# An encoder step in split fp32 products: input loaded in place, weights of the retention output loaded ahead, one tile with priority, the last products in a written order

## The chip, the cores and the metric

The kernel runs on one core of one Trainium2 chip. The core has five engines with instruction streams of their own: TensorE (PE), which multiplies matrices, VectorE (DVE), ScalarE (ACT), GpSimd (POOL) and SyncE (SP), which here issues most DMA transfers. They wait for one another through semaphores. The metric is the device time of one execution in microseconds (us). A kernel's time is the median of its runs.

## The reference

One step of a one-layer streaming encoder: 1024 prompt tokens and 64 sample tokens, width 1024. Cut to what matters:

```python
def mixer_prompt(h, g_attn, w_in, ...):
    rq, rk, rv, rg, sq, sk, sv, ga, gb = split(rms_norm(h, g_attn) @ w_in)
    q, k, v = retention_qkv(rq, rk, rv, pos)                  # rotary
    st, o = scan(retention_block, s0, chunks(q, k, v))        # 4 heads, chunks of 64
    swa_o = swa_attend(sq, band(sk), band(sv), bias, sinks)   # window 128
    a = (rms_norm(o) * silu(rg)) @ w_ret_out
    b = swa_o @ w_swa_out
    return (sigmoid(ga) * a + sigmoid(gb) * b) @ w_mix_out
...
h = h + mixer(h)                                    # prompt and sample, with their caches
h = h + cross_attn(rms_norm(h, g_cross), mk, mv)    # 4 heads, 256 memory tokens, then @ w_co
hn = rms_norm(h, g_ffn)
h = h + (silu(hn @ w_gate) * (hn @ w_up)) @ w_down  # D_FF = 2816
y = rms_norm(h, g_final)                            # h * rsqrt(mean(h*h) + 1e-6) * g_final
```

Everything is float32. Outputs are y for prompt and sample tokens, the retention states, the window's keys and values, and the memory's keys and values.

## The kernel before

**Products.** All 1088 tokens stand as columns (T = 1088; a half is 544, a quarter HC = 272; CH = 384, 384, 320). Activations are kept with features on the 128 partitions, so a unit of work is a 128x128 weight block against some hundred token columns. Each fp32 operand is split into a high part, cast to the type that TensorE takes (fp32r), and a low part, the rest: `split` (L122) is an ACT cast (L123) and a DVE subtraction (L124). A product is three matmuls, high by high, high by low, low by high (`mm3`, L147, and `multiply`, L199, lines 205, 206 and 208). The large products (in-projection, gate, up, down) are Strassen products (`strassen`): of a weight pair and operand blocks B11, B12, B21, B22 (features by token halves) seven products are made with sums T1 to T4 of the blocks; the weights' sums are made on POOL (`weight_ops`, L183 to L189).

**Order.** The instructions are written for all engines in one program, and a scheduler sets the order on each engine. `high_priority()` lets instructions pass others, `issue_after(x)` holds an instruction until x has been issued. SP issues loads and stores in order, and an entry that waits for a buffer holds what is behind it.

**Start** (`start_phase`, L403). The x columns are loaded by half and feature block, 16 pieces of 128x544, into the staging tile xr with four buffers; ACT multiplies each by the gain g into xg (L428). From xg `operands_early` splits B11 and B12, `operands_late` splits B21 and B22, and `first_sums` and `put_sum` (L1280) subtract on DVE and split T1 = B12 − B11, T2 = B22 − T1, T3 = T2 − B11 and T4 = B21 − T2, in place in xg's quarters. With w_v's blocks (`plain_weights`) the first products follow.

**Filler** (`filler`, L1042). While the window attention (SWA) runs, whose matmuls are small, this generator yields larger products between its steps. Its first loop (`operands`) loads the retention result d_gate[0], 8 feature blocks by three column chunks, each load held until `self.loaded`, the last weight load so far, and splits it into `rets`. Then come the last memory head's values, and then w_ret_out block by block: `unit` = `unit_raw` (a load of 512 KB into the staging tile "raw", two buffers) and `unit_parts` (the splits). The SWA's tokens are loaded after `operand_loaded`, the last load of the first chunk.

**Cross output** (`cross_out_phase`, L1219). For each block m of w_co and each chunk a dense product is added to the residual (L1241), stored, multiplied by the FFN's gain and the norm of before (L1244) into xg, and its squares are added into rstd_f (`add_square`, L278). After the last block the norm follows: a product with ones (L306), roots, and a product that spreads them over partitions (L330).

**Tail** (`down`, L1412). The last group of w_down's products leaves out P2 and P4 of the Strassen scheme; instead 16 plain products of 128x272 (nine matmuls each) are made at the end, eight for the first quarter of columns, eight for the second. Each is added to y (L1506) and passed to `complete` (L1441): square on ACT, add to rstd on DVE (L1450), multiply y by the final gain on ACT (L1451). After the first eight, `final_norm` is called for the second half (columns 544 to 1087) and for the first quarter, after the last eight for the second quarter: matmuls with ones (L306), roots on 128 x few columns (`rsqrt`, L284), a spreading product (L1527) and a copy (L1528). `final_scale` multiplies y by it on DVE (L1533) and stores.

## Time and profile before

| | |
|---|---|
| median of 3 runs | 2258.14 us (2256.48 to 2258.49) |
| the profiled execution | 2251.97 us |
| its span, first to last instruction | 2250.1 us |
| mean granted TensorE clock | 0.988 |
| PE busy, DVE busy | 97%, 71% of the span |
| bytes moved by DMA | 290.84 MB, mean 129 GB/s |

The profile is that of one execution. Busy time is given by engine; the matmuls' ends are modelled, so a busy PE isn't PE at its peak. In a group of instructions the row reads line, engine, operation, output and inputs, shapes and count, then busy time and mean ns of one, then the idle time of the engine ahead of them and what ended most of it. In a timeline the row begins with the start and the duration in us from the span's start. In the table of waits a row names what waited, what it waited for, the total in us, how often, and the longest. L12 is line 12 of the kernel.

### The profile page before, as it was taken

To read this page: it belongs to the slowest core of one execution; us is meant where nothing else is said; L and a number is where in the kernel's file an instruction comes from. 1 tells how busy PE (TensorE), PEld (TensorE's weight loads), DVE (VectorE), ACT (ScalarE), POOL (GpSimd) and SP (SyncE) were. 2 spreads that over 40 slices of the span, in tenths; PEclk is the share of its full clock that TensorE was granted. 3 is DMA by queue.
4 is the path that set the end of the run, shared out by engine and by line. 5 is a ranking of instruction groups with operands and counts; after the bars stand their busy time and mean duration, and the time that the engine had idled before them with its cause. 6 is when DMAs were issued, how large, how long until landed. Compare 5 with 4: busy or idle time off the path is not lost.

```text
span 2250.1 us, 41674 instructions
## 1 busy us (share of the span) xinstructions
PE 2172.4 (97%) x16382; PEld 2108.2 (94%) x16382; DVE 1594.2 (71%) x2656; ACT 896.2 (40%) x1921; POOL 689.0 (31%) x466
## 2 busy tenths in 40 slices
PE   7899999999999989999999999999999999999996
PEld 6899999999999977779999998999999999999996
DVE  8985878677687568875455565776777767777596
ACT  7333333435444355553233343333222223344344
POOL 1441534342253112220000000014555556434471
PEclk9999999999999989999999999999999999999997
DMA  5433344443445475326343111412342332475223
GB/s 199 159 120 109 111 129 130 132 130 113 169 139 187 143 242 164 111 67 222 121 153 113 39 66 59 143 62 91 122 148 79 101 131 85 152 258 192 86 84 108
DMA packets 182598, 290.84 MB, mean 129 GB/s; under 512 B 40290, under 2 KB 110850, under 8 KB 182402
## 3 DMA queue, kind: packets, MB, share of 16 engines
q1 hardware_dynamic: 177794, 279.26, 38.2%
q10 hardware_dynamic: 4608, 8.91, 1.1%
q8 instruction: 129, 2.11, 0.4%
q14 instruction: 67, 0.55, 0.1%
HBM read 196.95 MB, written 91.16 MB: 128 GB/s over the span
## 4 chain that ended last, share of the span: by engine, by line
PE 80%; DVE 10%; DMA 4%; issue 3%; ACT 2%; POOL 1%; SPq 0%; DVEq 0%; ACTq 0%; POOLq 0%
PE pq L205 15%; PE pq L208 15%; PE pq L206 15%; PE pd L149 8%; PE pd L150 8%; PE pd L151 8%; DVE wq L124 2%; PE pout L992 1%; PE pp L976 1%; DMA hl<-d_op 1%; PE pss L934 1%; DVE T L124 1%; DVE B L124 1%; PE pk L691 1%; DVE xg L1280 1%
## 5 line engine op out<-in xcount | busy, mean ns | idle before, releaser
L123 ACT CAST wq<-raw 128x512 fp32r<-128x512 f32 (+1 forms) x505 | 307.9, 614 | 572.1 <-PE pq L208 308.2
L124 DVE TENSOR_TENSOR wq<-raw,wq 128x512 fp32r<-128x512 f32 (+1 forms) x505 | 447.6, 890 | 107.7 <-ACT wq L123 105.7
L205 PE MATMUL pq<-T,wq 128*128 128x272 f32 x1832 | 501.3, 291 | 6.4 <-DVE u L252 3.1
L206 PE MATMUL pq<-T,wq 128*128 128x272 f32 x1832 | 497.7, 288 | 0.0
L205 PE MATMUL pq<-B,wq 128*128 128x272 f32 x1592 | 436.7, 292 | 11.7 <-ACT wq L123 10.5
L206 PE MATMUL pq<-B,wq 128*128 128x272 f32 x1592 | 435.1, 290 | 9.1 <-DVE B L124 8.9
L208 PE MATMUL pq<-T,wq 128*128 128x272 f32 x1832 | 382.6, 289 | 1.0 <-DVE wq L124 0.9
L183 POOL TENSOR_TENSOR raw<-raw 128x512 f32<-128x512 f32 (+1 forms) x59 | 81.6, 1383 | 899.7 <-DVE wq L124 615.2
L205 PEld LDWEIGHTS pq<-T,wq 128*128 128x128 f32 x1832 | 345.2, 188 | 7.2 <-DVE u L252 3.2
L206 PEld LDWEIGHTS pq<-T,wq 128*128 128x128 f32 x1832 | 348.5, 190 | 0.3 <-issue 0.3
L208 PE MATMUL pq<-B,wq 128*128 128x272 f32 x1592 | 333.5, 289 | 0.0
L206 PEld LDWEIGHTS pq<-B,wq 128*128 128x128 f32 x1592 | 304.4, 191 | 11.7 <-DVE B L124 11.3
L205 PEld LDWEIGHTS pq<-B,wq 128*128 128x128 f32 x1592 | 301.3, 190 | 12.4 <-ACT wq L123 10.5
L208 PEld LDWEIGHTS pq<-T,wq 128*128 128x128 f32 x1832 | 285.3, 188 | 2.4 <-DVE wq L124 1.7
L208 PEld LDWEIGHTS pq<-B,wq 128*128 128x128 f32 x1592 | 249.1, 189 | 0.5 <-issue 0.3
L252 DVE TENSOR_TENSOR u<-pq,u 128x544 f32<-128x544 f32 x177 | 127.7, 721 | 128.2 <-PE pq L208 127.5
L186 POOL TENSOR_TENSOR raw<-raw 128x512 f32<-128x512 f32 (+1 forms) x59 | 83.5, 1415 | 141.0 <-DVE wq L124 133.4
L563 DVE TENSOR_TENSOR stage<-pq,u 128x544 f32<-128x544 f32 x112 | 80.4, 718 | 29.1 <-PE pq L208 26.5
L962 POOL TENSOR_TENSOR t<-t,den 128x768 f32<-128x768 f32 (+2 forms) x34 | 47.9, 1409 | 167.5 <-DVE nm L950 58.7
L184 POOL TENSOR_TENSOR raw<-raw 128x512 f32<-128x512 f32 (+1 forms) x59 | 88.3, 1497 | 3.7
L1438 POOL TENSOR_TENSOR y<-u,y 128x544 f32<-128x544 f32 x38 | 63.0, 1664 | 73.6 <-DVE y L1436 51.8
L189 POOL TENSOR_TENSOR raw<-raw 128x512 f32<-128x512 f32 (+1 forms) x59 | 84.1, 1426 | 4.4
(356 smaller groups left out, 4669.8 us busy)
## 6 DMA issues: line engine op xcount, KB each, us to landing
hl<-d_op SPq DMA_DIRECT2D x85, 272.0 KB, 4.1
d_qkv<-stage SPq DMA_DIRECT2D x44, 272.0 KB, 2.1
d_op<-stage SPq DMA_DIRECT2D x44, 272.0 KB, 2.1
d_op<-ht SPq DMA_DIRECT2D x44, 272.0 KB, 3.3
raw<-w_gate SPq DMA_DIRECT2D x22, 512.0 KB, 3.4
raw<-w_up SPq DMA_DIRECT2D x22, 512.0 KB, 3.5
d_gate<-stage ACTq DMA_DIRECT2D x32, 272.0 KB, 2.3
raw<-w_down SPq DMA_DIRECT2D x16, 512.0 KB, 4.3
```

What stands on the lines that cost most here:

```text
L123: self.last_cast = self.nc.scalar.copy(hi, src).ins
L124: self.nc.vector.tensor_tensor(out=lo, in0=src, in1=hi.bitcast(F32), op=ALU.subtract)
L149: mm(ps, wh, xh, start=start, stop=False)
L150: mm(ps, wh, xl, start=False, stop=False)
L151: self.last_mm = mm(ps, wl, xh, start=False, stop=stop).ins
L184: tt(out=a21, in0=a21, in1=a22, op=add)
L186: tt(out=a11, in0=a22, in1=a11, op=sub)
L189: tt(out=a12, in0=a12, in1=a11, op=sub)
L205: mm(ps[:, c, :HC], w[:, 0, ks], x[:, 0, cs], start=start, stop=False)
L206: mm(ps[:, c, :HC], w[:, 0, ks], x[:, 1, cs], start=False, stop=False)
L208: self.last_mm = mm(ps[:, c, :HC], w[:, 1, ks], x[:, 0, c * HC:(c + 1) * HC], start=False, stop=stop).ins
L252: add = lambda out, a, b: nc.vector.tensor_tensor(out=out, in0=a, in1=b, op=ALU.add)
```

## The change

Four edits.

1. Start: the 16 pieces of x are loaded straight into xg, and ACT no longer multiplies them by g there. The operands B11 to B22 are made with the gain: high part = x times g on ACT, low part = x times g minus the high part in one DVE instruction (scalar_tensor_tensor). The sums take the gain in as well; gneg holds −g. `first_sums` isn't used here any more.
2. Filler: the load of w_ret_out's first block is written ahead of the loads of the retention operands; its splits stay where they were. As `unit_raw` sets `self.loaded`, the operands' loads are now held until this load.
3. Cross output: the last block's steps behind the product are emitted with high priority.
4. Tail: the last 16 products and everything behind them are written in `finish`, in a fixed order. `queued` holds each DVE instruction until the one before it in this list has been issued; `in_order` does the same for PE. The norm of the second half is taken during the first eight products and the following (sums after product 5, spread after 7), that of the first quarter after products 11 and 14. The final gain is no longer multiplied on ACT but by the scaling itself. For the second quarter the sum over partitions is written 128 rows wide (a product with a 128x128 of ones, over the accumulated squares and the last square), and the roots are taken on 128x272.

```diff
...
         self.last_cast = self.nc.scalar.copy(hi, src).ins
-        self.nc.vector.tensor_tensor(out=lo, in0=src, in1=hi.bitcast(F32), op=ALU.subtract)
+        return self.nc.vector.tensor_tensor(out=lo, in0=src, in1=hi.bitcast(F32), op=ALU.subtract).ins
...
         self.early = [sp.tile([P, 2, HC], F32, name=f"early{i}") for i in range(4)]
-        xr = lambda: sp.tile([P, HALF], F32, tag="xr", bufs=4, name="xr")
+        self.gneg = self.np.tile([P, KT], F32, name="gneg")
+        nc.vector.tensor_scalar(self.gneg, g, -1.0, None, ALU.mult)
         raws = [self.wp.tile([P, 1024], F32, tag="raw", bufs=2, name="raw") for i in range(2)]
...
             for k in range(k0, k0 + 4):
-                x = xr()
-                self.load(x, io["xT"][k, :, hs])
-                nc.scalar.mul(self.xg[k][:, hs], x, g[:, k:k + 1])
+                self.load(self.xg[k][:, hs], io["xT"][k, :, hs])
...
                 columns(n)
-            if n == 1:
-                self.operands_early()
         self.load(self.ident, io["c_ident"])
-        w = self.plain_weights(raws)
-        self.operands_late(self.first_sums)
-        return w
+        self.start_operands()
+        return self.plain_weights(raws)
+    def start_operands(self):
+        nc = self.nc
+        g, stt = self.gains[:, 0, :], nc.vector.scalar_tensor_tensor
+        self.op_tiles(0, ("B11", "T1"))
+        self.ops["B12"] = [self.b12[:, k] for k in range(4)]
+        self.op_tiles(1, ("B21", "B22", "T2", "T3"))
+        self.op_tiles(0, ("T4",))
+        col = lambda t, k: t[:, k:k + 1]
+        qs = [self.quarters(k) for k in range(4)]
+        for i, name in enumerate(("B11", "B12", "B21", "B22")):
+            for k in range(4):
+                o, x, gk = self.ops[name][k], qs[k][i], col(g, k + i // 2 * 4)
+                nc.scalar.mul(o[:, 0], x, gk)
+                stt(o[:, 1], x, gk, o[:, 0].bitcast(F32), ALU.mult, ALU.subtract)
+        for k, (b11, b12, b21, b22) in enumerate(qs):
+            nc.vector.tensor_tensor(out=b12, in0=b12, in1=b11, op=ALU.subtract)
+            nc.scalar.mul(b12, b12, col(g, k))
+            self.put_op("T1", k, b12)
+        for k, (b11, b12, b21, b22) in enumerate(qs):
+            stt(b12, b22, col(g, k + 4), b12, ALU.mult, ALU.subtract)
+            self.put_op("T2", k, b12)
+        for k, (b11, b12, b21, b22) in enumerate(qs):
+            stt(b11, b11, col(self.gneg, k), b12, ALU.mult, ALU.add)
+            self.put_op("T3", k, b11)
+        for k, (b11, b12, b21, b22) in enumerate(qs):
+            stt(b21, b21, col(g, k + 4), b12, ALU.mult, ALU.subtract)
+            self.put_op("T4", k, b21)
...
+            first = self.unit_raw(io["w_ret_out"][0], KT)
             for c0, n in CH:
...
             for m in range(KT):
-                u = self.unit(io["w_ret_out"][m], KT)
+                u = self.unit(io["w_ret_out"][m], KT) if m else self.unit_parts(first, KT)
                 for c0, n in CH:
...
                 ps = self.dense(u, self.couts, c0, n)
-                nc.vector.tensor_tensor(out=x, in0=ps, in1=x, op=ALU.add)
-                self.store(self.d_h[1][m, :, c0:c0 + n], x)
-                acc = self.rstd_f[:, c0:c0 + n]
-                nc.vector.scalar_tensor_tensor(self.xg[m][:, c0:c0 + n], x, self.gains[:, 2, m:m + 1],
-                                               self.rstd[:, c0:c0 + n], ALU.mult, ALU.mult)
-                self.add_square(acc, x, m == 0, cq, n)
+                with tc.high_priority() if m == KT - 1 else nullcontext():
+                    nc.vector.tensor_tensor(out=x, in0=ps, in1=x, op=ALU.add)
+                    self.store(self.d_h[1][m, :, c0:c0 + n], x)
+                    acc = self.rstd_f[:, c0:c0 + n]
+                    nc.vector.scalar_tensor_tensor(self.xg[m][:, c0:c0 + n], x, self.gains[:, 2, m:m + 1],
+                                                   self.rstd[:, c0:c0 + n], ALU.mult, ALU.mult)
+                    self.add_square(acc, x, m == 0, cq, n)
                 if m == KT - 1:
...
-    def operands_late(self, sums=None):
+    def operands_late(self):
         self.op_tiles(1, ("B21", "B22", "T2", "T3"))
...
             self.put_op("B22", k, b22)
-        if sums is not None:
-            sums()
         for k, (b11, b12, b21, b22) in enumerate(qs):
...
                 nc.vector.tensor_tensor(out=acc, in0=acc, in1=sq, op=ALU.add)
-            nc.scalar.mul(o, o, self.gains[:, 3, m:m + 1])
...
             q = self.rings[ring].tile("wb", slot=slots[m // 2 % 2])
-            self.split(raw[:, :2 * n], q[:, 0, :2 * n], q[:, 1, :2 * n])
+            self.last_queued = self.split(raw[:, :2 * n], q[:, 0, :2 * n], q[:, 1, :2 * n])
             rest += [(m + i, q[:, :, i * n:(i + 1) * n], self.ops[("B21", "T4")[i]]) for i in range(2)]
-        for c0 in (0, HC):
-            for m, q, xs in rest:
-                ps = self.ps.tile([P, 2, 512], F32, tag="q", name="pq")[:, 0, :HC]
-                for k, x in enumerate(xs):
-                    ks = slice(k * P, (k + 1) * P)
-                    x = x.rearrange("p a (b c) -> p a b c", b=2)[:, :, c0 // HC]
-                    self.mm3(ps, q[:, 0, ks], q[:, 1, ks], x[:, 0], x[:, 1], k == 0, k == len(xs) - 1)
-                v = y[m][:, c0:c0 + HC]
-                nc.vector.tensor_tensor(out=v, in0=ps, in1=v, op=ALU.add)
-                complete(m, c0, HC)
-            if c0 == 0:
-                self.final_norm(HALF, HALF)
-                self.final_scale(y, HALF, HALF)
-            self.final_norm(c0, HC)
-        for c0 in (0, HC):
-            self.final_scale(y, c0, HC)
-
-    def final_norm(self, c0, n):
+        self.finish(y, rest)
+    def queued(self, emit):
+        with self.tc.issue_after(self.last_queued):
+            self.last_queued = emit().ins
+    def finish(self, y, rest):
         nc = self.nc
-        acc = self.rstd[:, c0:c0 + n]
-        spans = self.spans(n)
-        with self.tc.high_priority():
+        tt, stt, ts = nc.vector.tensor_tensor, nc.vector.scalar_tensor_tensor, nc.vector.tensor_scalar
+        cols = [slice(0, HC), slice(HC, HALF), slice(HALF, T)]
+        squares, factors = {}, {}
+        bank = lambda: self.bank_pair()[:, 0, :]
+        def product(c, m, q, xs):
+            ps = bank()[:, :HC]
+            for k, x in enumerate(xs):
+                ks = slice(k * P, (k + 1) * P)
+                x = x.rearrange("p a (b c) -> p a b c", b=2)[:, :, c]
+                self.mm3(ps, q[:, 0, ks], q[:, 1, ks], x[:, 0], x[:, 1], k == 0, k == len(xs) - 1)
+            return ps
+        def grow(c, m, ps):
+            v = y[m][:, cols[c]]
+            self.queued(lambda: tt(out=v, in0=ps, in1=v, op=ALU.add))
+            sq = self.rstd[:, cols[c]]
+            if m:
+                sq = self.hl.tile([P, HALF], F32, tag="hl", name="sq")[:, :HC]
+            nc.scalar.activation(sq, v, AF.Square)
+            squares[c, m] = sq
+        def gather(c, m):
+            acc = self.rstd[:, cols[c]]
+            self.queued(lambda: tt(out=acc, in0=acc, in1=squares[c, m], op=ALU.add))
+        def sums(c):
+            spans = self.spans(cols[c].stop - cols[c].start)
+            ps = bank()[:, :2 * len(spans)].rearrange("p (t two) -> p t two", two=2)
+            for i, (a, w) in enumerate(spans):
+                a += cols[c].start
+                self.last_mm = nc.tensor.matmul(ps[:, i, :], self.rstd[:, a:a + w], self.ones[:, :2], start=True, stop=True).ins
             r = self.np.tile([P, 5], F32, tag="rf", bufs=2, name="rs_f")[:, :len(spans)]
-            self.token_rstd(r, [acc], spans, D)
-            for a, b in ((0, 2), (2, 5)) if n > 512 else ((0, len(spans)),):
-                pb = self.norm_psum("pb")
-                a0, a1 = spans[a][0], spans[b - 1][0] + P
-                for i in range(a, b):
+            factors[c] = r, spans, ps[:, :, 0]
+        def roots(c):
+            r, spans, ps = factors[c]
+            v = self.np.tile([P, 5], F32, tag="vf", bufs=2, name="rf_v")[:, :len(spans)]
+            t = self.np.tile([P, 5], F32, tag="tf", bufs=2, name="rf_t")[:, :len(spans)]
+            self.steps(r, v, t, ps)
+        def wide_roots(c, m):
+            ps = bank()[:, :HC]
+            mm = nc.tensor.matmul
+            mm(ps, self.ones, self.rstd[:, cols[c]], start=True, stop=False)
+            self.last_mm = mm(ps, self.ones, squares[c, m], start=False, stop=True).ins
+            v, t = (self.hl.tile([P, HALF], F32, tag="hl", name="wide")[:, :HC] for _ in range(2))
+            self.steps(self.rstd[:, cols[c]], v, t, ps)
+        def spread(c):
+            r, spans, _ = factors[c]
+            for part in ((0, 2), (2, 5)) if len(spans) > 4 else ((0, len(spans)),):
+                pb = bank()
+                a0, a1 = spans[part[0]][0], spans[part[1] - 1][0] + P
+                for i in range(*part):
                     at = spans[i][0] - a0
-                    nc.tensor.matmul(pb[:, at:at + P], r[:, i:i + 1].broadcast_to([P, P]), self.ident, start=True, stop=True)
-                nc.scalar.copy(acc[:, a0:a1], pb[:, :a1 - a0])
-
-    def final_scale(self, y, c0, n):
+                    self.last_mm = nc.tensor.matmul(pb[:, at:at + P], r[:, i:i + 1].broadcast_to([P, P]), self.ident,
+                                                    start=True, stop=True).ins
+                c0 = cols[c].start
+                nc.scalar.copy(self.rstd[:, c0 + a0:c0 + a1], pb[:, :a1 - a0])
+        def scale(c, k):
+            o = y[k][:, cols[c]]
+            self.queued(lambda: stt(o, o, self.gains[:, 3, k:k + 1], self.rstd[:, cols[c]], ALU.mult, ALU.mult))
+            self.store(self.io["o_y"][k, :, cols[c]], o)
+        for j in range(2 * KT):
+            c, m = divmod(j, KT)
+            ps = self.in_order(lambda: product(c, *rest[m]))
+            grow(c, rest[m][0], ps)
+            if (j - 1) % KT and j:
+                gather((j - 1) // KT, rest[(j - 1) % KT][0])
+            if j == 5:
+                self.in_order(lambda: sums(2))
+                roots(2)
+            if j == KT - 1:
+                self.in_order(lambda: spread(2))
+            if j == KT + 3:
+                self.in_order(lambda: sums(0))
+                roots(0)
+            if j == KT + 6:
+                self.in_order(lambda: spread(0))
+            if j >= KT:
+                scale(2, j - KT)
+        for k in range(3):
+            scale(0, k)
+        self.in_order(lambda: wide_roots(1, rest[-1][0]))
+        for k in range(3, KT):
+            scale(0, k)
         for k in range(KT):
-            o = y[k][:, c0:c0 + n]
-            self.nc.vector.tensor_tensor(out=o, in0=o, in1=self.rstd[:, c0:c0 + n], op=ALU.mult)
-            self.store(self.io["o_y"][k, :, c0:c0 + n], o)
+            scale(1, k)
+    def steps(self, out, v, t, ps):
+        nc = self.nc
+        stt, q = nc.vector.scalar_tensor_tensor, self.queued
+        q(lambda: nc.vector.tensor_scalar(v, ps, 1.0 / D, EPS, ALU.mult, ALU.add))
+        nc.scalar.activation(out, v, AF.Sqrt)
+        q(lambda: nc.vector.reciprocal(out, out))
+        q(lambda: nc.vector.tensor_tensor(out=t, in0=out, in1=out, op=ALU.mult))
+        q(lambda: stt(t, t, -0.5, v, ALU.mult, ALU.mult))
+        q(lambda: stt(out, t, 1.5, out, ALU.add, ALU.mult))
...
```

`in_order` is a method that the kernel has already; it holds PE's instructions behind `self.last_mm`.

2 lines of the change are left out of this document (1 added, 1 removed).

## The prediction

> **What bounds the kernel now.** I read the page's first part, then the waits of TensorE (PE) in the four places that the change touches, then a timeline of each.
>
> ```profile
> span 2250.1 us, 41674 instructions
> PE 2172.4 (97%) x16382; PEld 2108.2 (94%) x16382; DVE 1594.2 (71%) x2656; ACT 896.2 (40%) x1921; POOL 689.0 (31%) x466
> PE pq L205 <- ACT wq L123: 10.5, 1, 10.5
> PE pq L206 <- DVE B L124: 5.5, 3, 2.6
> PE pb L815 <- ACT ret_o L811: 5.1, 5, 1.4
> PE pd L149 <- ACT wq L123: 8.6, 2, 5.8
> PE pt L306 <- DVE rstd_f L278: 3.6, 1, 3.6
> PE pb L1527 <- DVE rs_f L294: 5.3, 3, 2.7
> ```
>
> PE is busy 97% of the span, so all that any change of order can give back is 2250.1 − 2172.4 = 77.7 us. The six rows of waits (total, times, longest) lie, in order, at 0–60 us (two rows), 120–560, 815–880, 1460–1540 and 2130–2251 us: the start, retention, the filler's output weights, the cross output and the tail. Each part of the change aims at one of them, the third row excepted. No matmul work is removed anywhere, so the gain cannot be more than these waits and what comes before and behind them.
>
> **Start.** The matmuls wait for operands, and VectorE (DVE) makes the operands.
>
> ```profile
> 5.00:10.00 5.00, 0.00 (x0) 0.00 (x0) 1.48 (x3) 4.99 (x9) 0.00 (x0) 1.00 0.94 312
> 80.00:90.00 10.00, 9.77 (x79) 9.77 (x79) 10.00 (x15) 3.58 (x6) 3.05 (x3) 1.00 0.46 158
> 5.64 1.39 ACT L428 ACTIVATE xg<-xr,gains 128x544 f32<-128x544 f32 x2
> 6.93 0.63 ACT L123 CAST B<-xg 128x544 fp32r<-128x544 f32 x1
> 7.59 0.72 DVE L124 TENSOR_TENSOR B<-xg,B 128x544 fp32r<-128x544 f32 x1 [6.58 <-ACT B L123]
> L124 DVE TENSOR_TENSOR T<-xg,T 128x544 fp32r<-128x544 f32 x16 | 13.5, 871 | 0.7 <-ACT T L123 0.7
> L124 DVE TENSOR_TENSOR B<-xg,B 128x544 fp32r<-128x544 f32 x12 | 9.7, 807 | 7.5 <-ACT B L123 7.5
> L124 DVE TENSOR_TENSOR b<-xg,b 128x544 fp32r<-128x544 f32 x4 | 2.9, 722 | 0.7 <-ACT b L123 0.7
> L269 DVE SCALAR_TENSOR_TENSOR xc<-ld,gains,xc 128x384 fp32r<-128x384 f32 x16 | 9.9, 619 | 11.0 <-ACT xc L268 11.0
> L124 DVE TENSOR_TENSOR mix<-ld,mix 128x384 fp32r<-128x384 f32 x16 | 8.9, 558 | 8.1 <-ACT mix L123 8.1
> ```
>
> In a table by slices the columns are PE, its loads, DVE, ACT and POOL, each busy us (instructions), then granted clock, DMA share and GB/s. DVE is the limit: once it runs, at 7.59, it is full, still 10.00 of 10.00 us at 80–90. So the stage shortens by what DVE gains, not by the 10.5 us that PE waits.
> - DVE begins sooner. Now ACT multiplies x by g (two in 1.39 us from 5.64), casts (6.93), and only then DVE subtracts (7.59). After, the product of x and g is itself the high part: the first DVE instruction follows one 0.7 us multiplication, at about 6.4. −1.2 us.
> - DVE idles less. The three L124 groups hold 0.7 + 7.5 + 0.7 = 8.9 us of idle time, of which 6.58 is the first wait: 2.3 are left, all behind ACT. ACT drops from 48 instructions on x (16 multiplications, 32 casts) to 36, and x no longer waits for four staging buffers. About 0.4 stays: −1.9 us.
> - DVE's instructions grow. The count stays 48 (32 splits, 16 subtractions), but 28 become scalar_tensor_tensor with a gain per partition: 16 for the B blocks, 4 each in the sums T2, T3, T4. At equal shape that form takes 619 against 558 ns: 28 × 0.061 = +1.7 us, and gneg once, about 0.1.
> - The built program's order puts two more retention instructions (about 0.7 us each) on DVE ahead of PE's wait near 98 us. They are only brought forward; this stands in the bound.
>
> Sum −1.2 − 1.9 + 1.8 = **−1.3**. Bounds: −3.6 (all idle goes, no surcharge) to +1 (1.2 of the idle stays, and the two instructions are not made good).
>
> **Retention, 110–560 us.** The start shifts how weights' products and retention are interleaved; no work changes. The third row of waits is what can move: a transposition (pb) waits for the norm of its head. There are 20 such places, five wait 1.0–1.4 us now. In the new order the number of matmuls between a head's last product and its pb falls from 89 to 68 at the first place and rises at thirteen of the others. I take 0, bounds −5.1 (none waits) to +5 (ten wait).
>
> **Filler.** The load of w_ret_out[0] moves ahead of the retention operands.
>
> ```profile
> 809.83 12.77 SPq L117 DMA_DIRECT2D swin<-d_gate  x7
> 831.35 0.81 SPq L117 DMA_DIRECT2D raw<-w_ret_out  x2
> 820.40 2.50 DVE L124 TENSOR_TENSOR wq<-raw,wq 128x512 fp32r<-128x512 f32 x4 [1.81 <-ACT wq L123]
> 831.58 0.27 PE L911 MATMUL pd<-ident,swin 128*128 128x128 f32 x1
> 837.65 0.69 PE L149 MATMUL pd<-ret,wq 128*128 128x384 f32 x1 [5.79 <-ACT wq L123]
> 842.33 0.52 PE L151 MATMUL pd<-ret,wq 128*128 128x384 f32 x1
> 845.15 0.34 PE L149 MATMUL pd<-ret,wq 128*128 128x384 f32 x1
> 820.00:825.00 5.00, 4.43 (x19) 4.14 (x20) 4.53 (x13) 4.91 (x11) 0.00 (x0) 0.50 0.90 283
> 825.00:830.00 5.00, 4.79 (x39) 4.52 (x38) 3.19 (x9) 2.75 (x12) 0.77 (x1) 0.89 1.04 384
> 830.00:835.00 5.00, 1.38 (x13) 1.05 (x13) 4.69 (x17) 4.27 (x19) 0.62 (x1) 0.79 0.93 330
> ```
>
> The load is issued at 831.35, because in the program it stands behind the loads of the gates; PE stands still for 5.79 us. After, the load stands near the head of SP's queue, but it needs a staging buffer that the split at 820.40 frees, at about 821.7. SP issues in order, so the seven gate loads that now go out from 809.83 to 822.6, and everything else behind, wait for it too: the one on which PE's next instruction depends (token v, transposed at 831.58) comes last. From 821.7 until then some 3.8 MB must come in (0.5 of weights, nine gate loads of 0.2, the window's queries 1.0, its keys and values 0.5). At the 330–384 GB/s of the last two slices that is 10–11.5 us: PE's transposition moves from 831.58 to about 834, and the output products, which follow it, start there and not at 837.65. **−2.8**, since the weights are long there. What is late next: DVE (4.69 of 5.00 busy at 830–835) with the gate splits. Bounds: −5 (the idle time falls to 2.4 us) and 0 (the splits that were covered by the stall are on the path).
>
> After the stall twelve matmuls run at half pace (0.52 us at 842.33, 0.34 at 845.15): 12 × 0.18 = 2.2 us that a shorter stall might save. A wait of 2.8 us (8.6 less 5.8 in the L149 row) ahead of 820.4 was followed by a granted clock of 0.50, so I count nothing for it. By the Trainium skill, "TensorE: Matmul & The Clock Gate", "What's actually happening", an idle window of some 3.4 us halves the clock, free-running; with 2.4 us left the sum would be about 2 us better by the rule; the trace's 2.8 us with a clock of 0.50 behind it speak against counting on it.
>
> **Cross output.** The 3.6 us wait on L278 has its cause on DVE, where the last tile's chain queues behind splits. In the built program the order on DVE, ACT and PE in this stage is the same as before, instruction by instruction: the priority is set on instructions that the tile's own products already release late. **0**, bounds −0.3 to +0.3.
>
> **Tail.** The last 16 products get a written order, with the norm of each third between them; scaling becomes one instruction; the last third's root is taken over the full width.
>
> ```profile
> 2217.84 1.17 PE L306 MATMUL pt<-ones,rstd 128*128 128x2 f32 x10
> 2225.19 1.62 PE L1527 MATMUL pb<-ident,rs_f 128*128 128x128 f32 x6 [2.68 <-DVE rs_f L294]
> 2226.46 0.57 PE L149 MATMUL pq<-B,wb 128*128 128x272 f32 x1
> 2236.51 0.29 PE L151 MATMUL pq<-T,wb 128*128 128x272 f32 x1
> 2244.12 3.55 SPq L120 DMA_DIRECT2D o_y<-y  x7
> 2224.96 1.35 DVE L1533 TENSOR_TENSOR y<-y,rstd 128x544 f32<-128x544 f32 x2
> 2243.56 2.55 DVE L1533 TENSOR_TENSOR y<-y,rstd 128x272 f32<-128x272 f32 x7
> L1533 DVE TENSOR_TENSOR y<-y,rstd 128x272 f32<-128x272 f32 x14 | 5.1, 437 | 0.0
> L787 PE MATMUL pos<-state,qsm 128*64 128x256 f32 x16 | 4.3, 392 | 0.0
> L1149 DVE RECIPROCAL cden<-cden 128x2 f32<-128x2 f32 x16 | 2.6, 165 | 8.5 <-ACT p L1147 8.5
> L291 DVE RECIPROCAL rtok<-rtok 128x8 f32<-128x8 f32 x1 | 0.2, 185 | 0.0
> ```
>
> - Between the two eights of products PE does no product from 2217.84 to 2226.46. Two of the three pb waits, 5.3 less the last one's 1.3, are there: 4.0 us, now filled by products. The second eight take 2236.79 − 2226.46 = 10.3 us, 1.4 over eight products of nine matmuls at full pace (9.77/79 = 0.124 each at 80–90 us, 8.9 in all), which a clock that stays up gives back. The last product ends at 2236.8 − 5.4 = 2231.4.
> - Behind it DVE is late: per product it now has an addition, a gathering of squares (2.55/7 = 0.36 each) and a wide scaling (1.35/2 + 0.06 = 0.73): 1.45 us against PE's 1.11, over eight 2.7 us, of which about half is made good where PE stops for the sums. Its last addition ends at 2233.0, the square at 2233.4, two wide fp32 matmuls (0.39 each at 256, so 0.45) at 2234.4. DVE meanwhile has a gathering, a wide scaling and three narrow ones (0.42): until 2235.3. Then 0.45 for the first step, 0.45 for the root on ACT, the reciprocal, three steps of 0.45.
> - A reciprocal 272 wide doesn't occur. From 2 to 8 wide it grows by 20 ns, 3.3 ns an element, so 0.165 + 270 × 0.0033 = 1.06 at most; at one element per cycle like the 437 ns row, 0.44. I take 0.75: the chain ends at 2235.3 + 0.45 + 0.45 + 0.75 + 1.35 = 2238.3.
> - The stores. Thirteen (five of the second third, eight of the last) are now queued behind that chain on SP, which issues one in 3.55/7 = 0.51 us; DVE needs only 0.42. First scaling ends 2238.7, last issue 13 × 0.51 later, 2245.4. From the last issue (2244.12 + 3.55 = 2247.67) to the end of the span (2250.1) it is 2.45 us today, so the end is 2247.9: **−2.2**. Bounds: −4.5 (DVE keeps up, reciprocal 0.44) to 0 (reciprocal 1.06 and 1.5 us more of backlog).
>
> The Trainium skill, "VectorE: DVE Perf Modes", "First, the fixed hardware budget", says that the reciprocal iterates its division with a repeat count of 8. At eight cycles an element my estimate from that page would be 2.3 us, and the tail −0.7 in place of −2.2. The two rows (20 ns for six elements) bear out less than half of that.
>
> **Sum.** −1.3 + 0 − 2.8 + 0 − 2.2 = −6.3 us. The execution that was profiled took 2251.97 us (its span of 2250.1 and 1.9 around it), so 2245.7; that one lies 6.2 below the median of the runs, 2258.14, from which the forecast is **2251.8 us**. A difference of 0.2%, 4.5 us, is about what a measurement can tell from none.
>
> **Rivals.**
> 1. *The filler gives nothing* (chance 0.15): the gate loads held behind the buffer land so late that DVE's splits become the bound, which shows as waits "ret L124". For it: DVE 4.69 of 5.00 busy. Against it: output products need only the first third of the splits. 2251.8 + 2.8 = 2254.6, which counts as no change.
> 2. *The tail is bound by DVE and SP* (0.12): the wide root and the thirteen stores behind it eat the 5.4 us that PE gains. For it: SP's 0.51 against DVE's 0.42. Against: by the sum the end loses only 3.2 of them. 2251.8 + 2.2 = 2254.0, on the edge.
> 3. *Slower: retention loses its cover* (0.10). Place: the 20 pb waits of L815. Price: 1.0 to 1.4 us each. DVE is full until past 100 us, and where splits come ahead of a head's norm each costs 0.6–0.9 us. Ten further waits (12 us) make it 2263.8; six (7 us) are the point from which the kernel is slower than before. Against it: at thirteen places the cover grows.
> 4. *Better than the sum* (0.18): the clock holds at the filler (−2), five pb waits shrink (−2.5), DVE's idle time in the start is gone (−1): 2251.8 − 5.5 = 2246.3.
> 5. *The change doesn't do what it says*: of the cross part this is the forecast already.
>
> **How the numbers follow.** The forecast itself has 0.45, with a range of 2248.5 to 2255. Faster by over 0.2% means below 2253.6: the forecast's 0.42 of 0.45, rival 4's 0.18, a half of rivals 1 and 2 (0.13): 0.73. Within 0.2%: the other half of these (0.14), the rest of the forecast and a part of rival 3: 0.19. Slower, above 2262.7: 0.08. The bounds of start (2.3), retention (5), filler (2.5) and tail (2.2), added in squares, give ±6.4; leaned to rival 4's side, which has more chance than rival 3, 2244 to 2257.5 holds 8 of 10.
>
> **What would show it.** In the profile after: first matmul near 8.9 and DVE's first split near 6.4; DVE groups on x with 28 scalar_tensor_tensor about 0.06 over the others; the L815 waits still near 5 us; one PE wait of 2–3 us near 832 and the first output product near 834; the wait on L278 still 3.6 us; no pb wait between the last products, the last product 5 us earlier than now against the span's end before, and the last store's issue some 14 us behind it. Wrong would be: a wide reciprocal above 1.1 us, the filler's wait as long as before, or retention waits above 10 us.

## The result, and the profile after

In shared runs on one chip the changed kernel takes **2272.61 us** (median of 6, 2271.84 to 2278.1), the kernel before 2259.95 us (median of 6, 2256.48 to 2264.74). The ratio is 1.006, 95% interval [1.0044, 1.0076]: slower by 0.6%, some 13.5 us. The forecast was 2251.8 us, faster. The profiled execution after took 2271.84 us, that of before 2251.97, less than any of these six runs: so the two traces lie 19.9 us apart, and some 6 us of that belong to the one fast execution of before.

First lines of the page of after, then some of its waits of PE (total, times, longest) in the stretches shown for before: 0–60 (two rows), 120–560 (three), 815–890 (two), 1480–1560, 2150–2271 us.

```profile
span 2270.1 us, 41632 instructions
PE 2181.6 (96%) x16374; PEld 2115.0 (93%) x16374; DVE 1597.6 (70%) x2656; ACT 880.2 (39%) x1886; POOL 691.7 (30%) x466
```

```profile
PE pq L205 <- ACT wq L123: 9.5, 2, 9.1
PE pq L208 <- DVE wq L124: 2.9, 1, 2.9
...
PE pkv L149 <- DVE vb L751: 9.1, 3, 8.2
PE pb L840 <- ACT ret_o L836: 2.8, 3, 1.0
PE pss L149 <- DVE kt L742: 2.2, 3, 1.1
...
PE pp L1001 <- POOL t L987: 4.7, 1, 4.7
PE pd L149 <- ACT wq L123: 1.9, 1, 1.9
...
PE pt L306 <- DVE rstd_f L278: 3.6, 1, 3.6
...
PE pq L1579 <- DVE rstd L1557: 2.2, 1, 2.2
```

The wait before the output products has shrunk from 5.8 to 1.9 us at most, the one in the cross output hasn't moved, and two new ones stand out: 8.2 us in retention on `vb`, and 4.7 us in the filler on the softmax's `t`. To see where the time went, take the moment at which PE begins the same amount of matmul work in both traces, counted from the start in columns of the operands that it has streamed; the difference is how far the kernel is behind the trace of before. The table gives it in us, at times of before's trace (e1 and so on are the experiments below; "end" is the difference of the spans).

| at | 240 | 300 | 400 | 800 | 860 | 1960 | 2170 | end |
|---|---|---|---|---|---|---|---|---|
| after | −1.9 | +3.3 | +12.9 | +13.9 | +19.2 | +22.0 | +23.3 | +20.0 |
| e1, start alone | −1.3 | +4.0 | +15.8 | +17.0 | +18.9 | +23.6 | +23.9 | +23.5 |
| e14, start, ten fillers | −1.3 | −1.3 | −1.5 | −1.4 | −2.1 | +1.3 | +1.3 | +2.1 |
| e16, after, ten fillers | −1.0 | −1.1 | −1.0 | 0.0 | +6.7 | +7.6 | +10.3 | +7.8 |
| e4, tail alone | +4.9 | +4.8 | +4.5 | +3.0 | +1.7 | +1.0 | +1.1 | −1.1 |

So after loses 15 us between 240 and 400, in retention, 5 at the filler, 4 bit by bit between 860 and 2170, and gains 3 in the tail. What costs the 4 us was not looked into; e14 and e16 lose 3.4 and 3.6 there too. Between 203 and 592 us the two kernels do the same matmuls in another order, so the lag inside that stretch is rough: +3.3 at 300, −0.2 at 350. (e4, e9 and e12, whose start is that of before, are 4.9, 2.6 and 0.8 us behind at 240: so much do single executions differ.)

**Retention at 365–380 us.** SP's and DVE's rows in the timeline of after (start, duration), then its slices, what DVE waited for, and its DMA issues (KB each, median us to landing); behind them the issues and SP's timeline of before.

```profile
363.50 0.67 SPq L120 DMA_DIRECT2D d_rb<-rb  x1
364.26 4.99 SPq L120 DMA_DIRECT2D d_qkv<-stage  x2
367.41 0.48 DVE L742 SCALAR_TENSOR_TENSOR kt<-pk,tok,kt 128x256 fp32r<-128x256 f32 x1
378.37 0.72 DVE L588 TENSOR_TENSOR stage<-pq,u 128x544 f32<-128x544 f32 x1 [10.47 <-DMA d_qkv<-stage]
```

```profile
370.00:375.00 5.00, 3.02 (x25) 2.80 (x23) 0.00 (x0) 0.00 (x0) 0.00 (x0) 1.00 0.90 94
375.00:380.00 5.00, 0.00 (x0) 0.00 (x0) 1.63 (x3) 0.47 (x1) 0.00 (x0) 0.82 0.97 267
380.00:385.00 5.00, 3.80 (x17) 3.80 (x18) 3.71 (x8) 1.93 (x4) 1.99 (x2) 0.50 0.65 231
```

```profile
DVE stage L588 <- DMA d_qkv<-stage: 10.5, 1, 10.5
...
DVE stage L588 <- DMA d_qkv<-stage: 2.9, 1, 2.9
```

```profile
d_qkv<-stage SPq DMA_DIRECT2D x2, 272.0 KB, 14.1
```

```profile
d_rb<-rb SPq DMA_DIRECT2D x1, 1024.0 KB, 13.4
d_qkv<-stage SPq DMA_DIRECT2D x2, 272.0 KB, 5.1
```

```profile
349.85 0.67 SPq L120 DMA_DIRECT2D d_rb<-rb  x1
356.12 0.37 SPq L117 DMA_DIRECT2D vf<-d_qkv  x1
361.06 0.33 SPq L120 DMA_DIRECT2D d_qkv<-stage  x1
```

The bias table (`bias_table`, 1 MB in 1024 rows of 1 KB) is stored to d_rb in both kernels, and takes 13.4 us: the DMA engines are at 0.90 and move 94 GB/s. Before, the next store of a stage buffer was issued 11 us behind it. After, two of them are issued 0.8 us behind it, and land after 14.1 us. The projections' results pass through a ring of stage buffers (`staged`); until a store has landed, DVE has no buffer. So DVE stands still for 10.5 us, PE for 8.2, and behind it the granted clock is 0.50. The second of the two DVE rows is the same wait, 2.9 us long, at 256 us: there a run of small waits begins, and PE idles 4.4 us between 250 and 300, against 1.0 before. Nothing in the edit touches any of this: the scheduler drew another order of projections and retention.

### The profile page after: what moved, and what is told of

It reads as the page before. It is cut to its first block, busy times and chain, and to the rows that moved or that the text cites. A ratio compares the mean times of both kernels' runs of the same rounds, so it can differ in the third digit from the quotient of the medians.

```text
span 2270.1 us, 41632 instructions
## 1 busy us (share of the span) xinstructions
PE 2181.6 (96%) x16374; PEld 2115.0 (93%) x16374; DVE 1597.6 (70%) x2656; ACT 880.2 (39%) x1886; POOL 691.7 (30%) x466
## 4 chain that ended last, share of the span: by engine, by line
PE 78%; DVE 12%; DMA 5%; issue 2%; ACT 2%; POOL 1%; SPq 0%; ACTq 0%; DVEq 0%; POOLq 0%
PE pq L206 15%; PE pq L205 15%; PE pq L208 14%; PE pd L149 7%; PE pd L151 7%; PE pd L150 7%; DVE wq L124 3%; DMA hl<-d_op 1%; PE pout L1017 1%; PE pp L1001 1%; PE pss L959 1%; DVE B L124 1%; DVE T L124 1%; DMA d_qkv<-stage 1%; DVE stage L588 1%
## 5 line engine op out<-in xcount | busy, mean ns | idle before, releaser
L205 PEld LDWEIGHTS pq<-T,wq 128*128 128x128 f32 x1832 | 348.1, 190 | 11.0 <-issue 4.5
L206 PEld LDWEIGHTS pq<-T,wq 128*128 128x128 f32 x1832 | 350.5, 191 | 0.4 <-issue 0.4
L205 PEld LDWEIGHTS pq<-B,wq 128*128 128x128 f32 x1592 | 300.9, 189 | 12.2 <-ACT wq L123 9.1
L208 PEld LDWEIGHTS pq<-T,wq 128*128 128x128 f32 x1832 | 293.3, 190 | 7.3 <-DVE wq L124 6.9
```

The source lines that it names most:

```text
L205: mm(ps[:, c, :HC], w[:, 0, ks], x[:, 0, cs], start=start, stop=False)
L206: mm(ps[:, c, :HC], w[:, 0, ks], x[:, 1, cs], start=False, stop=False)
L208: self.last_mm = mm(ps[:, c, :HC], w[:, 1, ks], x[:, 0, c * HC:(c + 1) * HC], start=False, stop=stop).ins
```

## The experiments

All ratios are to runs of the kernel before on the same chip, with 95% intervals; before's medians there were 2257 to 2260 us.

**One edit at a time.** e1 is the start edit alone, e3 the filler edit alone, e4 the tail alone: each the hunks of the diff above with these lines at their heart.

```diff
-                self.load(x, io["xT"][k, :, hs])                        e1
+                self.load(self.xg[k][:, hs], io["xT"][k, :, hs])
+            first = self.unit_raw(io["w_ret_out"][0], KT)               e3
+        self.finish(y, rest)                                            e4
```

> The start edit alone; filler, cross output and tail as before. In the profile of the changed kernel the lag of TensorE behind the kernel before is about -2 us at 250 us, then +5 us comes at 260-280 and +10 at 365-385. Theory 'start': all of this comes from the start edit, which shifts the retention against the products; the time is 11 to 14 us above before, with a wait of TensorE of about 8 us on vb near 380 us. Rival 'drawn anew': the order of the retention hangs on every edit, and the start edit alone does not have that wait: within 4 us of before.

> The early load of w_ret_out[0] alone; the rest as before. Theory 'SP held': the load waits about 12 us on SP for its buffer, the gate, query and key loads behind it start only then, DMA runs at a third in the meantime, and the attention gets its operands late: 4 to 7 us above before, with a wait of TensorE of 4-5 us on POOL's t some 30 us behind the last in-projection product. Rival 'the start did it': the loss at the filler in the changed kernel came from DVE or DMA work left over by the shifted start; alone the edit gains 2 to 3 us, as the prediction had it.

> The written order of the last products and norms alone; the rest as before. Theory (the prediction's tail term): the last product ends about 5 to 8 us earlier against the work done, the chain behind it is 6 us longer (13.5 against 7.4 us from the last matmul to the end), sum -2.2 us, so 1 to 4 us under before. Rival: in the changed kernel the 7.4 us stand against a backlog that came from the feed-forward part; alone the edit is within 1 us of before or above it.

Measured: e1 2276.43 us, **1.0080** [1.0068, 1.0092]; e3 2260.65, **1.0015** [1.0006, 1.0024]; e4 2250.50, **0.9967** [0.9956, 0.9979]. The start alone loses all of it and more, the filler edit loses a little, the tail gains more than expected. The three come to +0.62%, the whole change to +0.6%; that they agree is partly chance, as e16 shows.

**The table's store.** e2 is e1 with that store issued by ACT's queue; e5 is e1 with the table written later (at 624–666 us), in eight pieces.

```diff
-        self.store(self.d_rb.rearrange(...), rb.unsqueeze(1).broadcast_to([16, 64, 256]))
+        self.nc.scalar.dma_start(self.d_rb.rearrange(...), rb.unsqueeze(1).broadcast_to([16, 64, 256]))   e2
+        self.store(self.d_row, rb)                                                                        e5
+        self.table = [lambda i=i: self.store(dst[:, i * w:(i + 1) * w], ...) for i in range(8)]
...
+                    if act is AF.Silu and self.table:
+                        with self.tc.issue_after(self.last_store):
+                            self.table.pop(0)()
```

> The start edit alone, and the store of the bias table (d_rb) issued by ACT instead of SP; every other instruction stands in the same order as in e1_start. Theory 'transfer behind transfer': the two stage stores behind the table on SP's queue wait for its 1024 rows, DVE waits for their buffers and TensorE for DVE; on another queue they land in 2-4 us, the 8 us wait near 380 us is gone, and the time is 9 to 11 us under e1_start, 1 to 4 above before. Rival 'the table fills the DMA engines': the queue does not matter, all 16 engines are busy with the table for 13 us whoever issued it; the wait stays within 2 us and the time within 3 us of e1_start.

> The start edit alone, and the bias table's copies written in eight pieces of 128 KB from a row in DRAM, one behind each of eight stores of the gates near 700 us, instead of one store of 1 MB near 364 us. Theory 'transfer behind transfer': the stall of 9.6 us on vb and the half clock behind it in e1_start come from the 1 MB store ahead of the stage stores, whatever queue it has (in e2 it stood on another queue and 5 us of the stall were left). Without it there: no wait over 1.5 us between 350 and 400 us, the time 10 to 13 us under e1_start, 5 to 8 above before, the rest being what is lost at 260-280 us. Rival: stage buffers or loads of w_v stall DVE there anyway, or the pieces stall the gates as long: within 4 us of e1_start.

Measured: e2 2270.19, 1.0059 [1.0043, 1.0074]; e5 2265.81, 1.0037 [1.0025, 1.0049]. PE's wait on `vb` was 9.6 us in e1, 5.0 in e2, and is gone in e5. So SP's order is half of the stall: with the table on another queue the stage stores still share DMA engines that it fills (in e2 a DMA share of 0.85 to 0.89 at 365–375 us, and the two stores behind it land after 12.2 us). The small waits at 250–300 us stay in e5 (4.4 us of idle time).

**Is it the edit's work or the new order?** e7 has only the load in place, and the old splits. e13, e14 and e15 are e1 with 8, 10 and 12 useless DVE instructions, writes to an unused buffer.

```diff
-                x = xr()                                                e7
+                x = self.xg[k][:, hs]
...
             self.put_op("T1", k, b12)                                   e13 to e15
+        for i in range(10):
+            nc.vector.memset(self.early[3], 0.0)
```

> Of the start edit only the loading in place: x is loaded straight into xg and multiplied by g there; splits, sums and their order in the program as before. In the built order two stage stores follow the bias table's store at once, as in e1_start. Theory 'any shift of the start moves the retention onto the table': a wait of 6 to 10 us near 370 us, the time 7 to 16 us above before although DVE does the same work. Rival 'the gain in the splits': the loss comes from the longer instructions on DVE; this kernel has none of them and is within 4 us of before.

> The start edit alone, and eight useless DVE instructions (writes of a constant to an unused buffer, 128x544) in the middle of it. They only shift the stage by some 2 to 5 us, an estimate from the 0.165 us that such a write of 128x128 takes, and the scheduler draws a new interleaving. In the built program the two stage stores still stand directly behind the bias table's store. Theory 'the draw': what matters is which stores stand behind the table; the stall of 8 to 10 us near 370 us stays, and the time is like the start edit alone or up to 5 us above, 1.007 to 1.011 of before. Rival 'the shorter start collides': giving back the shift takes the stall away, 1.002 to 1.004. Rival 'its work': eight instructions more, 2 to 5 us more than the start edit alone.

> The same with ten useless DVE instructions in place of eight. Here the built program has, behind the table's store, the same entries as the kernel before: a load, one stage store, two loads, and only then the next two stage stores. Theory 'the draw': no wait above 3 us between 350 and 400 us, and although this kernel does more on DVE than the one with eight, it is 8 to 15 us faster than the start edit alone: 1.000 to 1.005 of before. Whether the small waits at 260 to 280 us are gone tells if they belong to the draw too. Rival 'its work': the same as with eight and half a us more.

> The same with twelve useless DVE instructions. In the built program the two stage stores stand directly behind the table's store again. Theory 'the draw': the stall of 8 to 10 us near 370 us is back, 1.007 to 1.012 of before, slower than the one with ten by 8 to 15 us. Rival 'more shift is better': like ten or faster.

Measured: e7 2279.02, 1.0092 [1.0078, 1.0106]; e13 2266.35, 1.0045 [1.0030, 1.0060]; e14 **2256.54, 1.000** [0.999, 1.001]; e15 2274.0, 1.0078 [1.0063, 1.0093]. e14's fillers in the groups of DVE (0–60 us), its waits of PE at 245–285 (two rows) and at 345–400 us, and SP's timeline; then the wait at 345–400 us and SP's timeline of e15.

```profile
L457 DVE MEMSET early<- 128x544 f32 x10 | 5.1, 512 | 1.0 <-DVE early L457 0.4 <-DMA xg<-xT 0.2
```

```profile
PE pb L842 <- ACT ret_o L838: 1.1, 1, 1.1
PE po L151 <- DVE ss L124: 0.8, 1, 0.8
...
PE po L151 <- DVE ss L124: 0.3, 1, 0.3
```

```profile
348.46 0.67 SPq L120 DMA_DIRECT2D d_rb<-rb  x1
354.75 0.37 SPq L117 DMA_DIRECT2D vf<-d_qkv  x1
359.68 0.33 SPq L120 DMA_DIRECT2D d_qkv<-stage  x1
```

```profile
PE pkv L149 <- DVE vb L753: 9.6, 1, 9.6
```

```profile
367.72 0.68 SPq L120 DMA_DIRECT2D d_rb<-rb  x1
368.49 5.04 SPq L120 DMA_DIRECT2D d_qkv<-stage  x2
```

With 5.1 us of useless work more than e1, e14 is 20 us faster, and both the stall and the small waits in retention are gone; with two further instructions they are back. In e14 the built order around the table's store is that of before; in e13 and e15 the stage stores stand right behind it again. That settles the cause: not the edit's work, but the order that the scheduler draws for the start it makes. In e13 the draw shows in the other direction, too: it is 7.0 us ahead at 240 us, and loses some 13 between 360 and 400, so that its time came out under the 1.007 to 1.011 expected of it.

**The filler.** e6 is e3 with the gate loads not held behind the early load; e10 is the whole change with this and e5's repair.

```diff
+            loaded = self.loaded
             first = self.unit_raw(io["w_ret_out"][0], KT)
+            self.loaded = loaded
```

> The early load of w_ret_out[0] alone, but without it becoming the load that the gate loads are held behind: five gate loads go out ahead of it, as before, and the others follow. Theory 'SP held': what cost time in e3_filler is the gate, query and key loads behind the waiting entry; with five of them (and their splits) ahead, SP waits from later on and the attention's operands come 1-3 us earlier than in e3: 2 to 5 us under e3_filler, 1 to 3 under before. Rival 'splits collide': the loss is the output weights' splits, which push the softmax steps back on DVE and ACT; then this kernel, with the same early weights, is within 1.5 us of e3_filler.

> The whole changed kernel with two repairs: the bias table's copies written late in eight pieces as in e5, and the early load of w_ret_out[0] not holding the gate loads as in e6. Theory 'two transfers out of place': the parts add up, the changed kernel's 13.5 us above before less 10.6 (e1 to e5) and 5.6 (e3 to e6): 1 to 5 us under before. Rival: the repairs do not add up, because with a late retention other waits come forward: 3 us above before or more.

Measured: e6 2255.04, **0.9992** [0.9982, 1.0001], e10 2258.04, 0.9994 [0.9985, 1.0003]. What SP waited for at 815–850 us in after, two slices of it (last three columns clock, DMA share, GB/s), behind them the slices of before in which PE is at the same work, 14 us earlier, and the timeline of after; then SP's wait and PE's wait in e6.

```profile
SPq L117 <- DVE wq L124: 14.0, 2, 12.0
```

```profile
825.00:830.00 5.00, 5.00 (x42) 5.00 (x42) 3.53 (x5) 1.10 (x2) 0.00 (x0) 1.00 0.36 98
830.00:835.00 5.00, 2.07 (x18) 1.50 (x16) 2.12 (x4) 2.19 (x5) 0.00 (x0) 1.00 0.30 113
```

```profile
811.00:816.00 5.00, 5.00 (x42) 5.00 (x41) 3.53 (x5) 1.05 (x2) 0.00 (x0) 1.00 0.57 137
816.00:821.00 5.00, 2.24 (x18) 1.66 (x16) 2.05 (x3) 2.17 (x5) 0.00 (x0) 0.82 0.48 146
```

```profile
820.50 1.31 SPq L117 DMA_DIRECT2D swin<-d_rb  x2
835.65 0.34 SPq L117 DMA_DIRECT2D raw<-w_ret_out  x1
850.33 0.69 PE L149 MATMUL pd<-ret,wq 128*128 128x384 f32 x1 [0.69 <-ACT swin L938]
870.97 1.12 PE L1001 MATMUL pp<-ident,t 128*128 128x128 f32 x4 [4.74 <-POOL t L987]
```

```profile
SPq L117 <- DVE wq L124: 1.3, 2, 1.0
...
PE pp L976 <- POOL t L962: 2.0, 1, 2.0
```

SP waits 12 us for the staging buffer, with every gate load behind it, and the DMA engines stand at 0.30–0.36, where before they were at 0.48–0.57 at the same work. Then all operands come at once (a DMA share of 0.96 and 1.07 at 840–850 us), and PE waits 4.7 us for the softmax; DVE, which makes the splits, is full just ahead of that wait and in it (5.00, 5.00 and 4.94 of 5.00 us at 855–870). That the splits hold the softmax up is argued from this, not tried by itself. With the gate loads free, e6 gives back some 5 us of e3.

**The tail.** e8 is e4 with every second of the last stores issued by ACT; e9 is e4 with a narrow root for the last third too, the scalings in its gaps. e11 and e12 are e4 and e9 with e6's filler.

```diff
+            if c == 1 and k % 2:                                        e8
+                self.nc.scalar.dma_start(to, o)
...
-        self.in_order(lambda: wide_roots(1, rest[-1][0]))               e9
+        self.in_order(lambda: sums(1))
+        roots(1)
...
+        self.in_order(lambda: spread(1))
```

> The written tail alone, with four of the last third's eight stores issued by ACT instead of SP; order on DVE and PE the same. In e4_tail the last scaling ends at 2244.96 and the last store is issued until 2246.51. Theory (the prediction's step): SP's 0.51 us a store is what ends last, so the end comes 1 to 1.6 us earlier than in e4_tail. Rival: landing a store takes as long wherever it is issued and the queue of stores overlaps it; within 0.5 us of e4_tail.

> The written tail alone, with the last third's root taken like those of the others (sums of 128x2, roots on 128x3, spread and copy) and the scalings of the second third put into the gaps. In e4_tail the wide reciprocal took 1.85 us, where the prediction had 0.75, and the wide chain from the last square to the last root 6.3 us. Theory 'the reciprocal is the mis-sized term': the narrow chain (about 1.1 us sums, 1.3 roots, 1.7 spread, 0.4 copy) is 1 to 2 us shorter and the scalings no longer stand behind it: 1 to 3 us under e4_tail. Rival: the clock of TensorE halves in the gap and the spread takes longer, and SP's queue ends last anyway: within 0.7 us of e4_tail.

> The written tail and the early load of e6_filler_free, with the start as before. Theory: the parts that gain are independent (they stand 1300 us apart): 8 to 11 us under before. Rival: the filler's gain in e6 was noise: as e4_tail, 6.5 to 8 us under before.

> As e11, with the narrow root of e9. Theory: 9 to 13 us under before, the difference to e11 being that of e9 to e4. Rival: no different from e11.

Measured: e8 2250.28, 0.9966 [0.9954, 0.9977]; e9 **2245.94, 0.9941** [0.9929, 0.9953]; e11 2248.89, 0.9948 [0.9936, 0.9960]; e12 2246.14, 0.9941 [0.9929, 0.9953]. A second queue for the stores gives nothing that can be told. The narrow root is better by 0.26% in e9 against e4, which ran on different chips; between e12 and e11, on one chip, the same edit is worth 0.07%, which can't be told from none. In the traces the tail from 2170 us on gains 2.2 us in e4 and 3.9 in e9 (−2.1 to −6.0), so the root gives 1.7 us, 0.08%; the rest of the 0.26% lies ahead of the tail. e4's root and last scalings on DVE, then e9's.

```profile
2236.32 1.85 DVE L1607 RECIPROCAL rstd<-rstd 128x272 f32<-128x272 f32 x1 [0.49 <-ACT rstd L1606]
2241.99 2.97 DVE L1573 SCALAR_TENSOR_TENSOR y<-y,gains,rstd 128x272 f32<-128x272 f32 x7
```

```profile
2233.39 0.17 DVE L1612 RECIPROCAL rs_f<-rs_f 128x3 f32<-128x3 f32 x1 [0.27 <-ACT rs_f L1611]
2236.96 2.97 DVE L1573 SCALAR_TENSOR_TENSOR y<-y,gains,rstd 128x272 f32<-128x272 f32 x7
```

**The whole change on the old draw.** e16 is the changed kernel with e14's ten instructions, e17 that with e6's filler and e9's tail.

> The whole change, and the ten useless DVE instructions in its start, which give the old order around the bias table's store again. Theory 'the parts add up': 1.0000 (start with ten) plus 0.0015 (filler) less 0.0033 (tail alone) makes 0.998 of before; 2253 to 2256 us where before runs at 2258, and neither the 8 us wait near 375 us nor the small waits at 260 to 280 us. Rival 'the tail alone was partly its build': only the 2.2 us of the tail that the trace of the whole change showed come, 1.000 to 1.001. Rival 'each shift draws anew': another stall somewhere, above 1.003.

> The same, with the filler's load that doesn't move the gate loads' start, and the last third's root narrow. By the parts: 1.0000 less 0.0008 (filler mended) less 0.0059 (narrow tail) is 0.993 of before, about the best kernel so far. If the narrow tail's gain is partly its build, 0.996 to 0.998.

Measured: e16 2259.65, 1.0009 [1.0000, 1.0018]; e17 2254.39, 0.9987 [0.9976, 0.9998]. In e16 retention loses nothing (−1.0 at 400, 0.0 at 800), so with the old draw the change would be the same as before, not slower; but neither kernel has the gain that e4 and e9 have, and e17 missed what its parts had promised, 0.993. The best versions are e9, the kernel before with a narrow, ordered tail, and e12, the same with e6's filler (both 0.9941).

## Why the prediction was wrong, step by step

- **Retention, the step that failed**: "no work changes", "I take 0, bounds −5.1 … to +5 (ten wait)". It counted one kind of wait, the transpositions (pb). Those fell, 5.1 to 2.8 us. What was not counted is who holds the stage buffers: in the trace of before, the table's store took 13.4 us and no stage store was near, and the built order of after put two of them right behind it. Retention cost 16 us in the trace of after (−1.9 to +13.9). Rival 3 had the place, and a wrong mechanism; its 2263.8 us lie 9 us under the result.
- **Start.** First split 6.32 (6.4 expected), first matmul 9.15 (8.9), and the surcharge, in the groups of after at 0–50 us, .779 − .714 = 0.065 us (0.061):

```profile
L451 DVE SCALAR_TENSOR_TENSOR B<-xg,gains,B 128x544 fp32r<-128x544 f32 x12 | 8.9, 779 | 3.8 <-ACT B L450 3.6
L453 DVE TENSOR_TENSOR xg<-xg 128x544 f32<-128x544 f32 x4 | 2.9, 714 | 0.0
```

  At 240 us the kernel is 1.9 ahead, e1 1.3, against the −1.3 of the sum. But e14, with 5.1 us more on DVE, has the same −1.3, and e13 −7.0: "the stage shortens by what DVE gains" is not what sets it. The draw decides here too, kernels with the start of before differ by 4 us at the same place (4.9 to 0.8), and the agreement proves little.
- **Filler.** The forecast put the first output product at 834 (3.65 us ahead of 837.65; why it counted only 2.8 of these it doesn't say). The product starts at 850.33, which is 836.4 less the 13.9 us by which the kernel is late there (+13.9 at 800). So the step came in part, and by the table's count the lag falls from +13.9 at 800 to +11.7 at 840, in e3 from +2.7 to +0.1. It is lost behind that: at 860 the lags are +19.2 and +7.1. So the sum −2.8 fell outside its bounds (−5 to 0): e3 +0.15%, 3.3 us. It priced the one wait that goes, not what the loads held on SP delay besides: the 4.7 us on POOL's softmax, in e3 5.4, before 0.9, and behind it a clock of 0.50 and 0.85 at 870–880. Rival 1 named the late splits and took them for no gain, not for a loss.
- **Cross output.** 0, and the wait on L278 is 3.6 us as before.
- **Tail.** −2.2 forecast, and from 2170 us on the trace of after gives −3.3 (+23.3 to +20.0), e16 −2.5, e4 −2.2; e1, e3 and e14, with the tail of before, move by up to 0.9 us there. The size holds, a term does not: the wide reciprocal took 1.85 us, not 0.75, beyond "1.06 at most", since the step from 2 to 8 wide doesn't extend to 272. The Trainium skill, "VectorE: DVE Perf Modes", "First, the fixed hardware budget", with its repeat count of 8, was nearer: my estimate from it was 2.3 us. That the size holds is partly luck: the last product ends at 2252.71, less 23.3 is 2229.4, and so 2 us before the 2231.4 of the sum, which makes good the 1.1 us of the reciprocal. The rows of the last third in after are below: sum over partitions, reciprocal, last scalings, last stores.

```profile
2254.89 0.73 PE L1579 MATMUL pq<-rstd,ones 128*128 128x272 f32 x2 [2.18 <-DVE rstd L1557]
2257.61 1.85 DVE L1632 RECIPROCAL rstd<-rstd 128x272 f32<-128x272 f32 x1 [0.49 <-ACT rstd L1631]
2263.28 2.97 DVE L1598 SCALAR_TENSOR_TENSOR y<-y,gains,rstd 128x272 f32<-128x272 f32 x7
2264.20 3.37 SPq L120 DMA_DIRECT2D o_y<-y  x7
```

## What to carry to other kernels

An edit at the head of a program that a scheduler orders redraws the order of all that follows: compare the built order around every long transfer and every ring of buffers, and try the edit with a few useless instructions in it, before any gain or loss is put down to it. A load that must wait for a buffer doesn't belong ahead of others on a queue that issues in order. And a part that is measured alone should be measured in the whole again, as e16 did.

## What the runs showed of the hardware

**Matmuls at full clock don't keep the same pace in all builds.** Slices of 100 us in the stretch of gate and up products, in which PE never waits; the first bracket counts PE's matmuls. Before, after and e4:

```profile
1650.00:1750.00 100.00, 100.00 (x798) 100.00 (x798) 72.47 (x86) 30.06 (x50) 54.54 (x38) 1.00 0.33 112
```

```profile
1650.00:1750.00 100.00, 100.00 (x799) 100.00 (x798) 72.29 (x88) 28.53 (x48) 53.61 (x37) 1.00 0.39 126
```

```profile
1650.00:1750.00 100.00, 100.00 (x806) 100.00 (x805) 71.22 (x85) 28.81 (x48) 56.07 (x39) 1.00 0.31 103
```

806 in place of 798 or 799, 0.9% more, with the same instructions, granted clock (1.00) and no wait. The same stretch of the other traces has 805 or 806 in e8, e9, e11 and e12 as well, and 798 or 799 in all the rest. So every kernel with the new tail and the old start has the fast pace; with the start edited too (after, e10, e16, e17) it is gone. It is not the chip: e1 to e4 ran on one. Nor is it a faster clock, for the products of 384 and 320 columns go the other way: 609 matmuls at 1060–1160 us before, 603 in e4. So more than half of e4's gain is not the tail's order: in the table it goes from +4.9 at 240 to +1.1 at 2170, and only 2.2 come in the tail itself; what it gains ahead of the tail is lost in e16. This fits e16's 1.0009 [1.0000, 1.0018]: 1.000 for e14, plus 0.0015 for the filler, less 0.0011 for a tail of 2.5 us, is 1.0004. What gives a build one pace or the other was not tried and stays open.

**A store in rows of 1 KB** fills the DMA engines at 94 GB/s for 13 us, where other stretches of this kernel reach 384 GB/s; stores of 272 KB behind it took 14.1 us, against 5.1. Whether the short rows make it slow, or that it reads from 16 partitions only, was not tried.
